# A recurrent block on 1024-column tiles: normalising ahead of the split, two-bank PSUM tiles, and pools of its own

## The chip, the cores and the metric

The kernel runs on one NeuronCore of a Trainium2 chip. Its engines are TensorE (PE; PEld is its weight load), VectorE (DVE), ScalarE (ACT) and GpSimd (POOL); SyncE (SP) issues the transfers. Time is device microseconds for one execution. Of the kernel before, three runs are known: 2192.54, 2199.36 and 2201.11 us, median 2199.36. One execution was profiled, with every instruction's start and duration.

## What is computed

Input is x, 1024 tokens of 1024 features, float32. There are two layers; each is a mixing step and an MLP, with RMSNorm ahead and a residual add behind. The change is in the first layer's mixing step, the recurrent block, and in what borders on it:

```python
def recurrent_block(x, w_in, conv_w, conv_b, w_gate, b_gate, lam, w_out):
    u = x @ w_in                                  # x already rmsnorm(x, g)
    gate, rec = u[..., :D_RNN], u[..., D_RNN:]
    rec = causal_depthwise_conv(rec, ...)         # 4 taps along the tokens
    h = rg_lru(rec, ...)
    return (jax.nn.gelu(gate) * h) @ w_out

# rg_lru, in 8 blocks of 128 features:
    r, i = sigmoid(x_block @ w_gate + b_gate), split in halves
    log_a = -8 * r * softplus(-lam);  a = exp(log_a)
    b = sqrt(-expm1(2 * log_a)) * (i * x)
    h[t] = a[t] * h[t-1] + b[t]                   # a scan along the tokens
```

The MLP is `square(relu(rmsnorm(h) @ w_up)) @ w_down`. The second layer has chunked band attention in place of the recurrent block.

## The kernel before

Features lie on the 128 partitions, tokens along the columns. A [1024 x 1024] matrix is 16 tiles of 128 x 512: k or j = 0 to 7 counts blocks of 128 features, h = 0, 1 the halves of the tokens. Every float32 product is made of three fp32r matmuls: an operand is split into a high part (ACT copies it to fp32r) and a low part (DVE or POOL subtracts), and `mm` (L321 to L323) adds high x high, high x low and low x high. A projection of one feature block is 8 k-blocks x 3 matmuls x 2 halves = 48 matmuls of 128x512. `split` (L334, L335 and, with a gain, L337, L338) splits data, `prepared` (L284, L287) the weights of the projections, `wsplit` (L732, L733) those of the MLP.

**The start** (`loads` to `first_blocks`) stands in a `manual_schedule` block: its order is written out by a small planner of the kernel (`Plan`), which starts chains of instructions as their inputs are due. x arrives as 16 tiles on SP's queue with pieces of the first two weights between them. Each tile is multiplied by the norm's gain and split as it lands (`halve`); POOL squares it. PE multiplies at once. The factor 1/rms (`R[h]`, kept negative) comes later (`rstd`) and is put on the products as they leave PSUM, so PE need not wait for it.

**The blocks.** For each n, `rec_proj` makes the recurrent half's projection, one 512-column PSUM bank per half, and a DVE instruction takes it to SBUF times -R (L556), three columns of carry ahead (L553, L555). `conv` does one tap on ACT (L572) and three on DVE (L577) per half. `gates` does the two gate products and sigmoid, tanh and exp on ACT; `lru` does the arithmetic on DVE, two products on POOL (L597, L615), a square root on ACT and the scan (L617), the second half from the first's last column. `gelu_gate` makes the other projection two blocks later, scales (L629), applies gelu, multiplies by the scan's result (L631) and splits it to `Y[n]`. `next_w` takes a prepared weight and prepares ahead. Here, and everywhere outside the `manual_schedule` blocks, the framework's planner orders each engine's instructions from the program's order, the dependences and its own cost model, and it gives each tile a buffer of its pool.

**Pools.** `gp` has 66 tiles of 128x512, `sp` 10, `wp` 16 for split weights and 8 for raw ones, `ps1` the eight PSUM banks under four tags. They are open from the first instruction to the last.

**Behind the blocks**, `Out.whole` makes the eight output blocks: a load of the residual (`first`, L674 adds it), a store of the sum to `x1d`, the square and sum for the next norm (`last`, L368 and L374), and, for each pair of blocks, `combine`, which makes the seven operand combinations `XT[0]` to `XT[6]` of the MLP. The MLP's two products are done with seven multiplications in place of eight, in 2x2 blocks. `mlp_up` asks for R first (`o.r`, whose sums on PE are L352, L353), then works through 16 steps q; `mlp_down` goes through its seven products n in the order 0, 1, 5, 4, 6, 2, 3, 16 steps q each, with operands reloaded from DRAM (`hid`), adds finished PSUM banks to x (L851), and calls `finish` on tiles that are complete. In the first layer `finish` stores x to `x2d`, squares it, adds it to the norm's sum and splits it (`done1`); in the second it only stores the output. `mlp_up`, `mlp_down` and `combine` serve both layers.

## Time and profile before

| what | value |
|---|---|
| median of three runs | 2199.36 us (2192.54 to 2201.11) |
| the profiled execution | 2197.24 us, its span 2195.5 us |
| mean granted TensorE clock | 0.983 |
| start, until the first two projections are complete | 0 to about 48 us |
| the eight blocks and the output projection | to about 347 us |
| MLP of layer 1 | to about 950 us |
| attention | about 1000 to 1500 us |
| output projection and MLP of layer 2 | to the end |

The span goes from the first to the last instruction, and some 1.7 us of the execution's time lie outside it. A stretch of the profile gives the busy time of each engine with its count of instructions; matmuls are pipelined, so their durations overlap (each is recorded with 0.39 us and more) and it is the count in a stretch that tells PE's rate. A group of instructions has the line in the kernel, the tile written, the tiles read, the shapes and the count, then busy time, mean duration in ns, and the idle time of that engine just before them with what ended it. L numbers are lines of the kernel before.

### The profile page before, as it was taken

The page shows a single profiled execution, that of the slowest core. Times are in us where ns is not written, and L with a number is a line of the kernel's source. Part 1 is how long each engine was busy: PE and PEld are TensorE (multiplying, and loading weights), DVE is VectorE, ACT ScalarE, POOL GpSimd, SP SyncE. Part 2 cuts the span into 40 slices and gives each one's busy share as a digit, 9 for nine tenths or more (in the row PEclk, how much of TensorE's full clock was granted, in tenths as well). Part 3 has the DMA queues.
Part 4 walks back from the last instruction along what each step waited for, and adds up shares of the span by engine and source line. Part 5 has one row for each costly group of instructions (what it writes and reads, how often), then busy time and mean ns, then how long its engine had stood idle before and what let it go on. Part 6 is the DMA issues. An engine that isn't in the chain of part 4 may idle for free.

```text
span 2195.5 us, 29616 instructions
## 1 busy us (share of the span) xinstructions
PE 2113.9 (96%) x9753; PEld 1741.9 (79%) x9753; DVE 1583.7 (72%) x2716; ACT 1115.1 (51%) x2030; POOL 659.8 (30%) x567
## 2 busy tenths in 40 slices
PE   7898898999999999998999999999999999999999
PEld 5676686888888888776888888878788888888887
DVE  7788867777777775554777777777677777777843
ACT  4576745443444544444666666675443443444632
POOL 5454311333320000105666656651223333000000
PEclk8999999999999999999999999999999999999999
DMA  5111144444459774343333333353354444977733
GB/s 178 37 48 37 37 141 134 163 149 149 154 196 328 241 257 134 125 144 94 90 85 87 80 80 88 92 174 111 97 184 156 152 146 153 336 262 240 255 103 99
DMA packets 176746, 319.21 MB, mean 145 GB/s; under 512 B 20816, under 2 KB 23120, under 8 KB 176592
## 3 DMA queue, kind: packets, MB, share of 16 engines
q1 hardware_dynamic: 176592, 317.33, 44.6%
q8 instruction: 76, 1.25, 0.2%
q14 instruction: 78, 0.64, 0.1%
HBM read 219.73 MB, written 78.64 MB: 136 GB/s over the span
## 4 chain that ended last, share of the span: by engine, by line
PE 77%; DVE 11%; DMA 4%; issue 3%; ACT 3%; POOL 2%; SPq 1%; DVEq 0%; POOLq 0%; ACTq 0%
PE pj L321 11%; PE pj L322 11%; PE pj L323 11%; PE tp L322 6%; PE tp L321 6%; PE tp L323 6%; PE sc L321 4%; PE sc L322 4%; PE sc L323 4%; PE tp L1172 2%; DVE c L577 2%; PE po L1200 1%; DVE l L335 1%; DMA s<-in_xT 1%; PE po L1199 1%
## 5 line engine op out<-in xcount | busy, mean ns | idle before, releaser
L321 PE MATMUL pj<-h,wh 128*128 128x512 f32 x1269 | 509.9, 402 | 8.9 <-ACT h L334 4.4
L322 PE MATMUL pj<-l,wh 128*128 128x512 f32 x1269 | 497.4, 392 | 2.9 <-DVE l L338 2.0
L323 PE MATMUL pj<-h,wl 128*128 128x512 f32 x1269 | 496.7, 392 | 0.0
L732 ACT ACTIVATE wh<-raw 128x512 fp32r<-128x512 f32 x352 | 221.6, 630 | 339.0 <-PE po L322 81.4
L733 DVE TENSOR_TENSOR wl<-raw,wh 128x512 fp32r<-128x512 f32 x352 | 277.0, 787 | 116.6 <-ACT wh L732 113.2
L321 PEld LDWEIGHTS pj<-h,wh 128*128 128x128 f32 x1269 | 239.9, 189 | 56.0 <-ACT h L334 4.9
L323 PEld LDWEIGHTS pj<-h,wl 128*128 128x128 f32 x1269 | 239.4, 189 | 51.4
L322 PEld LDWEIGHTS pj<-l,wh 128*128 128x128 f32 x1269 | 240.3, 189 | 45.8 <-DVE l L338 2.9
L321 PE MATMUL tp<-h,wh 128*128 128x512 f32 x657 | 258.4, 394 | 5.0 <-ACT h L334 4.4
L322 PE MATMUL tp<-l,wh 128*128 128x512 f32 x657 | 258.4, 393 | 2.9 <-DVE l L335 2.8
L323 PE MATMUL tp<-h,wl 128*128 128x512 f32 x657 | 257.8, 392 | 0.0
L321 PE MATMUL sc<-h,wh 128*128 128x512 f32 x569 | 224.6, 395 | 6.8 <-DVE rec L556 6.8
L322 PE MATMUL sc<-l,wh 128*128 128x512 f32 x569 | 223.9, 393 | 3.0 <-DVE l L335 3.0
L323 PE MATMUL sc<-h,wl 128*128 128x512 f32 x569 | 223.6, 393 | 0.0
L765 POOL TENSOR_TENSOR raw<-raw,raw 128x512 f32<-128x512 f32 x32 | 52.2, 1631 | 396.1 <-DVE wl L733 374.9
L335 DVE TENSOR_TENSOR l<-raw,h 128x512 fp32r<-128x512 f32 x224 | 153.2, 694 | 22.2 <-ACT h L334 20.8
L747 ACT ACTIVATE s<-s 128x512 f32<-128x512 f32 x128 | 80.3, 629 | 170.1 <-DVE s L746 170.1
L334 ACT ACTIVATE h<-raw 128x512 fp32r<-128x512 f32 x224 | 136.6, 620 | 52.9 <-DMA raw<-hid 30.9
L321 PEld LDWEIGHTS tp<-h,wh 128*128 128x128 f32 x657 | 124.7, 190 | 32.2 <-ACT h L334 5.2
L322 PEld LDWEIGHTS tp<-l,wh 128*128 128x128 f32 x657 | 124.8, 190 | 31.1 <-DVE l L335 4.8
L287 POOL TENSOR_TENSOR wl<-raw,wh 128x512 fp32r<-128x512 f32 x74 | 105.6, 1433 | 134.2 <-ACT wh L284 133.4
L323 PEld LDWEIGHTS tp<-h,wl 128*128 128x128 f32 x657 | 124.7, 190 | 26.6 <-DVE wl L733 0.6
(262 smaller groups left out, 3971.0 us busy)
## 6 DMA issues: line engine op xcount, KB each, us to landing
hid<-s SPq DMA_DIRECT2D x224, 256.0 KB, 2.0
raw<-hid SPq DMA_DIRECT2D x224, 256.0 KB, 3.7
raw<-in_w_down SPq DMA_DIRECT2D x192, 256.0 KB, 3.5
raw<-in_w_up SPq DMA_DIRECT2D x128, 256.0 KB, 2.6
s<-in_w_down SPq DMA_DIRECT2D x64, 256.0 KB, 4.4
raw<-in_w_kv SPq DMA_DIRECT2D x32, 256.0 KB, 3.5
raw<-in_w_in SPq DMA_DIRECT2D x31, 256.0 KB, 3.1
od<-ev SPq DMA_DIRECT2D x48, 128.0 KB, 2.3
```

What stands on the lines that cost most here:

```text
L287: eng.tensor_tensor(wl, raw, wh.bitcast(F32), ALU.subtract)
L321: pe.matmul(ps, lhsT=wh, rhs=xh, start=start, stop=False, skip_group_check=more)
L322: pe.matmul(ps, lhsT=wh, rhs=xl, start=False, stop=False, skip_group_check=more)
L323: pe.matmul(ps, lhsT=wl, rhs=xh, start=False, stop=stop, skip_group_check=more)
L334: act.activation(h, src, AF.Copy)
L335: dve.tensor_tensor(l, src, h.bitcast(F32), ALU.subtract)
L577: dve.scalar_tensor_tensor(ct, rec[h][:, k : k + H2], vec[:, V_CW + k, n : n + 1], ct, ALU.mult, ALU.add)
L732: act.activation(wh, raw, AF.Copy)
L733: dve.tensor_tensor(wl, raw, wh.bitcast(F32), ALU.subtract)
L747: act.activation(out, out, AF.Square)
L765: pool.tensor_tensor(raw[A11], raw[A11], raw[A21], ALU.add)
L1172: pe.transpose(pt[:, g * P : (g + 1) * P], sc[:, (kb - kb0) * P : (kb - kb0 + 1) * P], ident)
```

## The change

- The start squares the tiles on ACT, sums them on DVE as they come, and makes R of a half before that half is split. `halve` then multiplies x by R on DVE and splits the result with the gain (`gneg`, since R is negative). Three projections are made there instead of two: the recurrent blocks 0 and 1, and the gelu side of block 0. Third and further weights are loaded when the first ones are split.
- The blocks work on 1024 columns in one instruction. Their tiles come from `bp` (10 tiles of 128x1024), PSUM from `ps2` (four tiles of two banks), weights from `wpa` (10 split, 4 raw). Convolution and gelu read PSUM themselves; the scaling by R, the carries and the copies to `rec` are gone. The "+1" in `lru` goes from DVE to ACT. The scan is one instruction. The gelu side follows its block in the same step. The gelu weights' low parts are subtracted on DVE instead of POOL.
- `WideOut` is the output projection of this block on the same pools: 1024-column residual loads, squares and stores.
- These pools are closed then, and `sp`, `wp` and `ps1` are opened on the same memory, with waits tile by tile.
- `combine` splits `XT[0]` and `XT[1]` first and has one copy less. `mlp_up` asks for R after the fifth product of its first step. `mlp_down` calls `finish` for a complete product only when the operands of the first four steps of the next product stand in the program (`DEFER`).

```diff
+NB = 10
+NRAW_A = 4
+NW_A = 10
 BANKS = {"pj": 2, "tp": 3, "po": 1, "sc": 2}
-LAG = 2
-EARLY = 1
 PIN = 0
-SQA = ((6, 1), (7, 1))
 WARM = 9
-BEHIND = {(0, 0): 0, (0, 2): 1, (0, 4): 1, (1, 0): 3, (1, 4): 5}
+FIRST = 3
...
+DEFER = 3
...
-    sp = ctx.enter_context(tc.tile_pool(name="sp", bufs=NS))
-    wp = ctx.enter_context(tc.tile_pool(name="wp", bufs=NW))
     tp = ctx.enter_context(tc.tile_pool(name="tp", bufs=12))
-    ps1 = ctx.enter_context(tc.tile_pool(name="ps1", bufs=1, space=bass.MemoryType.PSUM))
     dp = ctx.enter_context(tc.tile_pool(name="dp", bufs=1, space=bass.MemoryType.DRAM))
+
+
+    first_stage = ExitStack()
+    bp = first_stage.enter_context(tc.tile_pool(name="bp", bufs=NB))
+    wp = first_stage.enter_context(tc.tile_pool(name="wpa", bufs=NW_A))
+    ps2 = first_stage.enter_context(tc.tile_pool(name="ps2", bufs=4, space=bass.MemoryType.PSUM))
+    sp = ps1 = None
+    nraw = NRAW_A
...
+    def bf(s="b", dt=F32):
+        return bp.tile([P, T], dt, tag="b", name=nm(s))
+
+    def bank2():
+        return ps2.tile([P, T], F32, tag="p", name=nm("p"))
...
-    wlist = [(w_in[NF + n], None, dve if n < 3 else pool) for n in range(max(3, 1 + EARLY))]
-    for n in range(1, NF):
-        if max(3, 1 + EARLY) <= n + EARLY < NF:
-            wlist.append((w_in[NF + n + EARLY], None, pool))
-        if n >= LAG:
-            wlist.append((w_in[n - LAG], None, pool))
-    wlist += [(w_in[n], None, pool) for n in range(NF - LAG, NF)]
+    wlist = [(w_in[NF], None, dve), (w_in[NF + 1], None, dve), (w_in[0], None, dve)]
+    for n in range(1, NF + 1):
+        if 2 <= n + 1 < NF:
+            wlist.append((w_in[NF + n + 1], None, pool))
+        if n >= 2:
+            wlist.append((w_in[n - 1], None, dve))
     wlist += [(w_out[j], None, dve) for j in range(NF)]
...
+        q = xsq[k, h] = bf("acc")[:, hs(0)]
+        act.activation(q, xin[k, h], AF.Square)
+        yield plan.use("act", c_act(H2))
+        if k:
+            yield squared[k - 1, h]
+            dve.tensor_tensor(xsq[0, h], xsq[0, h], q, ALU.add)
+            plan.use("dve", c_dve(H2))
+        squared[k, h].set(plan.t)
...
-        yield weighed[1, NF - 1]
-        yield halved[NF - 1, h]
-        a = xsq[0, h]
-        for k in range(1, NF):
-            yield squared[k, h]
-            dve.tensor_tensor(a, a, xsq[k, h], ALU.add)
-            yield plan.use("dve", c_dve(H2)) - LAT
-        yield plan.t + LAT
-        ss = bank("po")
-        pe.matmul(ss, lhsT=ones, rhs=a, start=True, stop=True)
-        yield plan.pe(4 * H2)
+        yield squared[NF - 1, h]
+        if h == 0:
+            dve.tensor_scalar(gneg, vec[:, V_AN, :], -1.0, None, ALU.mult)
+        ss = bank2()[:, hs(h)]
...
+        R[h] = r
+        normal[h].set(plan.use("dve", c_dve(H2)))
+
+    def halve(k, h):
+        yield normal[h]
+        if k:
+            yield halved[k - 1, h]
+        x = xin[k, h]
+        dve.tensor_tensor(x, x, R[h], ALU.mult)
+        yield plan.use("dve", c_dve(H2))
+        hi, lo = gr("h"), gr("l")
+        g = gneg[:, k : k + 1]
+        act.activation(hi, x, AF.Copy, scale=g)
+        X[k][h] = (hi, lo)
+        halved[k, h].set(plan.use("act", c_act(H2)))
+        yield plan.t + c_act(H2) + LAT
+        dve.scalar_tensor_tensor(lo, x, g, hi.bitcast(F32), ALU.mult, ALU.subtract)
         plan.use("dve", c_dve(H2))
-        R[h] = r
-        if h == 1:
+        if (k, h) == (NF - 1, 1):
...
+        for x in range(FIRST):
+            first_ps[x] = bank2()
         for h in range(2):
-            for x in range(2):
-                first_ps[x, h] = bank(("pj", "tp")[x])
-            if h == 0:
-                order = [(x, k) for b in range(2) for x in range(2) for k in range(4 * b, 4 * b + 4)]
-            else:
-                order = [(x, k) for k in range(NF) for x in range(2)]
-            for x, k in order:
-                yield weighed[x, k]
-                yield halved[k, h]
-                mm3(first_ps[x, h], [w[1:] for w in first_w[x]], X, h, (k,))
-                yield plan.pe(3 * H2) - LAT
+            for k in range(NF):
+                for x in range(FIRST):
+                    yield weighed[x, k // 4]
+                    yield halved[k, h]
+                    yield plan.t + c_dve(H2) + LAT
+                    mm3(first_ps[x][:, hs(h)], [w[1:] for w in first_w[x]], X, h, (k,))
+                    yield plan.pe(3 * H2) - LAT
...
+    def project(w):
+        ps = bank2()
         for h in range(2):
+            mm3(ps[:, hs(h)], w, X, h)
+        return ps
...
+    def conv(n, ps):
+        c = bf("c")
+        act.activation(
+            c, ps, AF.Identity,
+            scale=vec[:, V_CW + 3, n : n + 1], bias=vec[:, V_CB, n : n + 1],
+        )
+        for k in range(3):
+            d = 3 - k
+            dve.scalar_tensor_tensor(
+                c[:, d:], ps[:, : T - d], vec[:, V_CW + k, n : n + 1], c[:, d:], ALU.mult, ALU.add
             )
-            for k in range(1, 4):
-                dve.scalar_tensor_tensor(
-                    ct, rec[h][:, k : k + H2], vec[:, V_CW + k, n : n + 1], ct, ALU.mult, ALU.add
-                )
-            c.append(ct)
-            cs.append(split(ct))
-        return c, cs
-
-    def gates(n, gw, c, cs):
-        r, i, t = [], [], []
-        for e, dst, vb in ((0, r, V_BR), (1, i, V_BI)):
+        ch, cl = bf("ch", F32R), bf("cl", F32R)
+        act.activation(ch, c, AF.Copy)
+        dve.tensor_tensor(cl, c, ch.bitcast(F32), ALU.subtract)
+        return c, ch, cl
...
+    def gates(n, gw, c, ch, cl):
+        sig = []
+        for e, vb in ((0, V_BR), (1, V_BI)):
+            ps = bank2()
             for h in range(2):
-                ps = bank()
-                mm(ps, (gw[0][:, e, :], gw[1][:, e, :]), cs[h], True, True)
-                s = gf("sig")
-                act.activation(s, ps, AF.Sigmoid, bias=vec[:, vb, n : n + 1])
-                dst.append(s)
-        for h in range(2):
-            tt = gf("tanh")
-            act.activation(tt, r[h], AF.Tanh, scale=sp4[:, n : n + 1])
-            t.append(tt)
-            pool.tensor_tensor(i[h], i[h], c[h], ALU.mult)
-        for h in range(2):
-            act.activation(r[h], r[h], AF.Exp, scale=sp8[:, n : n + 1])
+                mm(ps[:, hs(h)], (gw[0][:, e, :], gw[1][:, e, :]), (ch[:, hs(h)], cl[:, hs(h)]), True, True)
+            s = bf("sig")
+            act.activation(s, ps, AF.Sigmoid, bias=vec[:, vb, n : n + 1])
+            sig.append(s)
+        r, i = sig
+        t = bf("tanh")
+        act.activation(t, r, AF.Tanh, scale=sp4[:, n : n + 1])
+        pool.tensor_tensor(i, i, c, ALU.mult)
+        act.activation(r, r, AF.Exp, scale=sp8[:, n : n + 1])
+        act.activation(r, r, AF.Identity, bias=ones[:, 0:1])
         return r, i, t
...
+        u = bf("q")
+        dve.scalar_tensor_tensor(u, t, 1.0, r, ALU.add, ALU.mult)
+        dve.scalar_tensor_tensor(u, u, 4.0, r, ALU.subtract, ALU.mult)
+        act.activation(t, t, AF.Sqrt, scale=0.25)
+        dve.tensor_scalar(r, u, -0.5, -1.0, ALU.mult, ALU.add)
+        dve.scalar_tensor_tensor(t, t, -1.0, u, ALU.mult, ALU.mult)
+        pool.tensor_tensor(t, t, i, ALU.mult)
+        dve.tensor_tensor_scan(u, r, t, 0.0, ALU.mult, ALU.add)
+        return u
+
+    def gelu(ps):
+        g = bf("ge")
+        act.activation(g, ps, AF.Gelu_apprx_tanh)
+        return g
+
+    def gated(n, g, hid):
+        dve.tensor_tensor(g, g, hid, ALU.mult)
+        Y[n] = [split(g[:, hs(h)]) for h in range(2)]
...
+    recs = [first_ps[0], first_ps[1]]
+    gws = {0: gate_weights(0)}
+    g0 = gelu(first_ps[2])
+    prev = (gws.pop(0), *conv(0, recs[0]))
+    for n in range(1, NF + 1):
+        if 2 <= n + 1 < NF:
+            recs.append(project(next_w()))
         if n < NF:
-            rec, gw = recs[n]
-            prev = (gw, *conv(n, rec))
-        if n > 0:
-            HS[n - 1] = lru(*rit)
-        if LAG <= n < NF:
-            gelu_gate(n - LAG)
-    for n in range(NF - LAG, NF):
-        gelu_gate(n)
+            gws[n] = gate_weights(n)
+        rit = gates(n - 1, *prev)
+        if n < NF:
+            prev = (gws.pop(n), *conv(n, recs[n]))
+        hid = lru(*rit)
+        g = g0 if n == 1 else gelu(project(next_w()))
+        gated(n - 1, g, hid)
...
-            b12, b21, b22 = sf(), sf(), sf()
+            (b12, b22), (t1, t3) = self.scratch(), self.scratch()
+            self.XT[0][i] = split(x11, ga)
+            self.XT[1][i] = split(x21, gb)
             act.activation(b12, x12, AF.Copy, scale=ga)
-            act.activation(b21, x21, AF.Copy, scale=gb)
             act.activation(b22, x22, AF.Copy, scale=gb)
-            self.XT[0][i] = split(x11, ga)
-            self.XT[1][i] = split(b21)
-            t1 = sf()
             dve.scalar_tensor_tensor(t1, x11, ga, b12, ALU.mult, ALU.subtract)
             self.XT[4][i] = split(t1)
             dve.scalar_tensor_tensor(t1, t1, -1.0, b22, ALU.mult, ALU.subtract)
             self.XT[5][i] = split(t1)
-            dve.tensor_tensor(b12, b22, b12, ALU.subtract)
-            self.XT[6][i] = split(b12)
             self.XT[2][i] = split(b22)
-            dve.scalar_tensor_tensor(t1, t1, -1.0, b21, ALU.mult, ALU.subtract)
-            self.XT[3][i] = split(t1)
+            dve.tensor_tensor(t3, b22, b12, ALU.subtract)
+            self.XT[6][i] = split(t3)
+            dve.scalar_tensor_tensor(t1, x21, gb, t1, ALU.mult, ALU.add)
+            self.XT[3][i] = split(t1, -1.0)
...
+    class WideOut(Out):
+
+
+        def scratch(self):
+            b = bf("sc")
+            return b[:, hs(0)], b[:, hs(1)]
+
+        def whole(self, Z, j0):
+            ws, pss, xs = {}, {}, {}
+            acc = bf("acc")
+            for j, h in out_order(j0):
+                if j not in ws:
+                    ws[j], pss[j] = next_w(), bank2()
+                    xs[j] = bf("xr")
+                    dma(xs[j], self.resid[j])
+                mm3(pss[j][:, hs(h)], ws[j], Z, h)
+                x = xs[j][:, hs(h)]
+                dve.tensor_tensor(x, pss[j][:, hs(h)], x, ALU.add)
+                self.XR[j][h] = x
+                if h == 0:
+                    continue
+                dma(self.keep[j], xs[j])
+                if j == 0:
+                    act.activation(acc, xs[j], AF.Square)
+                else:
+                    q = bf("sq")
+                    act.activation(q, xs[j], AF.Square)
+                    if j < NF - 1:
+                        dve.tensor_tensor(acc, acc, q, ALU.add)
+                    else:
+                        for g in range(2):
+                            self.norm.acc[g] = gf("acc")
+                            dve.tensor_tensor(self.norm.acc[g], acc[:, hs(g)], q[:, hs(g)], ALU.add)
+                if j % 2:
+                    self.combine(j // 2)
...
-        R = [o.r(0), o.r(1)]
+        R = []
...
+            if not R:
+                R.extend((o.r(0), o.r(1)))
...
+                if q == DEFER:
+                    for j0, h in left:
+                        finish(j0, h)
+                    left = []
...
-                finish(0, 0)
+                left.append((0, 0))
...
-                finish(4, 1)
+                left.append((4, 1))
             elif n == 2:
                 add(Y, 0, 1, ALU.add)
-                finish(0, 1)
+                left.append((0, 1))
...
-    o1 = Out(xT, 0, x1d)
+    o1 = WideOut(xT, 0, x1d)
     o1.whole(Y, 0)
+
+
+    first_stage.close()
+    sp = ctx.enter_context(tc.tile_pool(name="sp", bufs=NS, reuse_waits="tile"))
+    wp = ctx.enter_context(tc.tile_pool(name="wp", bufs=NW, reuse_waits="tile"))
+    ps1 = ctx.enter_context(tc.tile_pool(name="ps1", bufs=1, space=bass.MemoryType.PSUM, reuse_waits="tile"))
+    nraw = NRAW
```

148 lines of the change are left out of this document (42 added, 106 removed).

## The prediction

> **What bounds the kernel now.** I read the page first, then the busy time of each engine by stretches, then the costs of single instructions in the stretches the change touches.
>
> ```profile
> span 2195.5 us, 29616 instructions
> PE 2113.9 (96%) x9753; PEld 1741.9 (79%) x9753; DVE 1583.7 (72%) x2716; ACT 1115.1 (51%) x2030; POOL 659.8 (30%) x567
> 0.00:58.00 58.00, 45.95 (x156) 33.60 (x157) 45.72 (x63) 26.30 (x43) 32.41 (x34) 0.85 0.51 174
> 93.50:253.00 159.50, 141.49 (x587) 111.94 (x586) 138.27 (x180) 113.21 (x162) 75.04 (x46) 0.97 0.11 36
> 0.00:347.50 347.50, 309.01 (x1268) 243.67 (x1269) 278.83 (x393) 208.82 (x311) 130.10 (x95) 0.96 0.25 83
> 349.00:372.00 23.00, 16.34 (x53) 12.08 (x54) 15.99 (x23) 13.57 (x24) 5.64 (x4) 0.85 0.31 97
> 372.00:640.00 268.00, 268.00 (x1183) 221.69 (x1182) 205.14 (x275) 109.78 (x187) 91.30 (x56) 1.00 0.46 157
> 882.00:900.00 18.00, 13.33 (x46) 10.00 (x45) 17.14 (x28) 14.65 (x28) 1.50 (x2) 0.81 0.69 232
> 928.00:950.00 22.00, 16.73 (x63) 12.86 (x62) 16.18 (x26) 12.22 (x22) 0.00 (x0) 0.84 0.61 200
> 1572.00:1602.00 30.00, 23.96 (x77) 16.88 (x76) 20.71 (x32) 17.68 (x31) 6.82 (x4) 0.83 0.38 124
> ```
>
> In the window rows the columns are the stretch, its length, busy time and count of PE, PEld, DVE, ACT and POOL, the granted clock, DMA share and GB/s. PE at 96% says little, since its matmuls overlap; the counts say more. From 372 to 640 PE is never idle and does 1183 matmuls in 268 us: 0.2265 us each. That is my unit, and a stretch loses its length minus count times 0.2265. The recurrent block with its output projection is 1248 products of 128x512 (16 projections of 48, 8 gate pairs of 12, 8 output blocks of 48), 283 us of PE. With 9 idle warm-up matmuls and about 11 others these are the 1268 of the row that ends at 347.5 us, so **some 64 us are lost before 347.5**: 58 - 143 x 0.2265 = 26 us in the start, 159.5 - 587 x 0.2265 = 27 us in the 159.5 us of steady blocks, the rest around them (13 of the 156 are warm-up and norm). In the steady blocks DVE is 87% busy (138.27 of 159.5), ACT 71%, and PE waits for DVE. Four short stretches lose more: 11.0 us (349 to 372), 7.6 (882 to 900), 7.7 (928 to 950), 12.6 (1572 to 1602). Everywhere else that the change reaches PE is full, and nothing can be won.
>
> **The change, part 1: the block's instructions.** These rows price it (groups of 60 to 275 us with shapes apart, L453 from the start; the three rows with slashes give the shortest, median and longest):
>
> ```profile
> L577 DVE SCALAR_TENSOR_TENSOR c<-rec,vec,c 128x512 f32<-128x512 f32 x48 | 44.4, 926 | 1.0 <-ACT c L572 0.3
> L617 DVE TENSOR_TENSOR_SCAN q<-sig,q,tanh x8: 1267/1704/2336, 95.9 to 267.7; 128x512 f32<-128x512 f32 x8
> L615 POOL TENSOR_TENSOR tanh<-tanh,sig x16: 1257/1741/2221, 92.2 to 264.9; 128x512 f32<-128x512 f32 x16
> L556 DVE SCALAR_TENSOR_TENSOR rec<-sc,rneg x5: 659/682/691, 77.8 to 201.6; 128x512 f32<-128x512 f32 x5
> L613 DVE TENSOR_SCALAR sig<-q 128x512 f32<-128x512 f32 x16 | 6.1, 418 | 0.0
> L453 DVE TENSOR_TENSOR w<-raw,w 128x256 fp32r<-128x256 f32 x2 | 0.8, 414 | 0.0
> L335 DVE TENSOR_TENSOR l<-s,h 128x512 fp32r<-128x512 f32 x16 | 10.9, 680 | 0.0
> L562 ACT ACTIVATE gw<-graw 128x256 fp32r<-128x256 f32 x6 | 2.4, 402 | 0.0
> L334 ACT ACTIVATE h<-c 128x512 fp32r<-128x512 f32 x16 | 10.1, 631 | 41.2 <-DVE c L577 41.2
> L572 ACT ACTIVATE c<-rec,vec 128x512 f32<-128x512 f32 x15 | 12.0, 801 | 0.0
> L595 ACT ACTIVATE tanh<-sig,sp 128x512 f32<-128x512 f32 x16 | 11.0, 732 | 4.8 <-DVE q L617 2.6 <-POOL tanh L615 2.1
> L591 ACT ACT_TABLE_LOAD x8 | 10.3, 1283 | 0.1
> ```
>
> No row shows 1024 columns, so I extend the slope. DVE takes 0.414 us for 256 columns and 0.68 for 512, so 1.2 for 1024 (bounds 1.06, the slope without a fixed part, and 1.36, twice a 512). ACT: 0.402 and 0.631, so 1.09; 1.26 for the L572 kind, 1.2 for the L595 kind. The scan: 1.27 at best for 512, so 2.5.
>
> Per block DVE loses the two scalings of rec, the two of gelu, the carries, the "+1" (to ACT) and half of all fixed costs. What stays: convolution 3 x 1.2, split of c 1.2, q twice 1.2, r 0.7, tanh x q 1.2, scan 2.5, gating 1.2, two splits 1.4, its share of weight splits 1.0: **15.2 us**, where 138.27 us over 587/108 = 5.4 blocks of matmuls make 25 now. The convolution gains twice: today it reads two SBUF tensors and takes 926 ns on average, while the form that reads PSUM (L556) never leaves 659 to 691. ACT per block: 1.26 + two sigmoids 2.4 + tanh and exp 2.4 + the "+1" 1.1 + three of 1.09 + two splits 1.25 + four table loads 5.1 + weights 2.4: **19.2 us**. POOL: two 1024-wide products, 4 x 1.26 = 5.0, plus weights at the same price 2.6: 7.6 us, since seven of the thirteen remaining projections' lower parts move to DVE (in its 1.0).
>
> How much may they take? The first three projections come out of the start, so by the end of the last gate projection PE owes 1248 - 144 - 384 = 720 matmuls, 163 us, and 84 more (19 us) of the first two output blocks need no last Y. That is 182 us for eight blocks, 22.8 each. DVE (15.2) and ACT (19.2) are both below, and four two-bank tiles suffice when the convolution reads rec within a block. So PE sets the pace. Waits that remain (weights in 10 buffers rather than 16, ACT at 84%) I put at 10 us in all; bounds 3 and 34 (the last if each block took the 24.5 us of its 108 matmuls on ACT too: the last Y at 57 + 196 + 10 = 263, 24 past its cover at 57 + 182 = 239).
>
> **Part 2: the start.** Normalising first means PE gets nothing until the whole first half is summed.
>
> ```profile
> GB/s 0 0 147 270 257 295 292 249 188 169 227 314 401 402 402 415 399 388 391 388 382 388 377 375 375 382 391 377 391 388 295 148 0 0 0 0 0 0 0 0
> 48.13 0.87 PE po L493 x2
> 51.85 0.65 DVE rneg L505
> 42.94 0.43 PE tp L321
> 43.36 0.43 PE tp L322
> ```
>
> The transfers of the first 30 us, in slices of 0.75 us, bring the eight first-half tiles and the three weight pieces queued between them (11 of 256 KB, 2.9 MB) by 11.7 us. Then a square and an add (0.63 + 0.69), sum to finished norm 52.5 - 48.13 = 4.4 us, scaling and split 1.4: 18.8, and about 20 since the second half's squares (now on ACT, 0.63 each) mix in. Today PE's first product starts at 5 us. But its data trickle in; from 20 us PE has three blocks on each tile (9 matmuls, 2.0 us) against 1.4 us of DVE, with no POOL work beside it. It starts cold: after a long wait today matmuls come every 0.43 us (42.94, 43.36) for some 15 matmuls, +3 us. So 144 products end at 20 + 3 + 32.6 = 55.6, say 57 (bounds 54 and 63, the latter with all eight second-half squares ahead of the norm on ACT and the cold start doubled). Today 143 are done at 58: no gain, no loss.
>
> Stage end: 57 + 1104 x 0.2265 + 10 = **317 us against 347.5: -30** (bounds -41 and 0).
>
> **Part 3: after it.** At 1572 to 1602 the sums of squares stand ahead of the first products in PE's order (three waits there, one of the first output stage, one DMA issue):
>
> ```profile
> PE sc L352 <- ACT ah L346: 2.6, 1, 2.6
> PE po L352 <- ACT ah L346: 1.3, 1, 1.3
> PE pj L322 <- DVE l L338: 1.5, 1, 1.5
> DVE xr L674 <- DMA s<-in_xT: 15.1, 8, 2.8
> raw<-in_w_up SPq DMA_DIRECT2D x128, 256.0 KB, 2.6
> ```
>
> The change asks for R only after the fifth product and drops the copy b21. The two waits of 3.9 us go, with most of the half-speed stretch behind them; the 1.5 us wait stays. Of 12.6 us I take **-7** (bounds -2 and -10). The same loss at 349 to 372 is 11.0 us, but here new pools open on the memory of the old: the first w_up loads must wait for the tiles that lie there, and some of these live to the last combine. The residual, for which DVE waits 15.1 us today, comes in eight loads of 512 KB into ten wide tiles, early enough. I take **-4** (bounds -9 and +6; the latter if two raw tiles load only after the last combine, a 2.6 us transfer, a GpSimd add and a split later).
>
> DEFER: before the 882 us stall ACT looks like this.
>
> ```profile
> 846.37 6.11 SPq L222 DMA_DIRECT2D raw<-hid  x6
> 850.28 0.62 ACT L334 ACTIVATE h<-raw 128x512 fp32r<-128x512 f32 x1
> 881.64 0.63 ACT L368 ACTIVATE acc<-x 128x512 f32<-128x512 f32 x1 [1.36 <-DVE x L851]
> 886.33 4.25 ACT L334 ACTIVATE h<-raw 128x512 fp32r<-128x512 f32 x8
> PE tp L321 <- ACT h L334: 4.4, 1, 4.4
> ```
>
> The next product's operands are issued by 852.5, yet ACT splits none between 851 and 886: the squares and splits of finish stand first in the order, and those wait for the adds after PE's last matmul. PE then waits 4.4 us and runs half-cold. With finish behind four operands (4 x 12 matmuls, 10.9 us of PE), its eight DVE instructions (5.4 us) fit; its four x2d stores go behind these operands on SP, and nobody reads them before the attention layer. Of 7.6 + 7.7 = 15.3 us I take **-13** (bounds 0, if the order stays as it is, and -15).
>
> Sum: -30 - 7 - 4 - 13 = -54. The profiled execution took 2197.24 us (2 below the median): **2143 us**.
>
> **The rivals.**
>
> *A. Another engine sets the block's pace (0.18).* For: ACT needs 19.2 of 22.8 us, its queue is in order, and DVE and POOL stretch each other: L615 goes from 1257 to 2221 ns, L617 from 1267 to 2336. If a DVE operation with two SBUF tensors never ran beside POOL, DVE's 11 us of these and POOL's 7.6 make 18.6, still under 22.8; against: it takes further waits. At 25.5 us a block Y ends at 57 + 204 = 261, 22 past its cover at 239 instead of the 10 allowed: 2155 us. The Trainium skill (SBUF — State Buffer, section "SBUF: two separate sides") speaks for this case: the port pair that VectorE and GpSimd share is an exclusive lock held for a whole instruction, so a 1024-wide POOL product could block DVE twice as long as now. The trace agrees as far as L617's 2336 against 1267 ns shows.
>
> *B. The order edits do not do what they say (0.13).* Operands stay behind finish (0 for -13), the new pools cost 6 (for -4), R gives only -2 (for -7): +28, 2171 us. For: where instructions fall is a planner's choice; against: the 35 us in which ACT could have split and did not.
>
> *C. Slower: PE waits for a PSUM tile in every block (0.07).* Only four tiles exist; rec keeps one until all of its convolution has read it. If a projection must wait for the two sigmoids and the convolution (2.4 + 1.26 + 3.6, with hand-overs 8 us) in each of eight blocks, that is 64 us: 2143 + 64 = 2207. It turns the sign from 54/8 = 6.8 us a block. Against: rec is finished a whole projection (10.9 us) and more before its tile is asked for again.
>
> **How the numbers follow.** The forecast has 0.62. All favourable bounds together give 2197 - 75 = 2122; A and B lie at 2155 and 2171, so the range is 2118 to 2182, which leaves out C and mixtures of A with B. A measurement of this kernel tells about 0.5% from no change (2188 to 2210). Faster 0.87, within 0.06, slower 0.07.
>
> **What would show it.** Right: first product near 20 us and from then on few idle places on PE; about 1260 matmuls done by 317; DVE below 70% in the steady blocks with convolution at 1.2 us; h<-raw splits before PE ends a product of mlp_down; no 4.4 us wait at its seams. Wrong: PE waiting for conv or sigmoid in each block (C), Y later than the first two output blocks (A), w_up transfers issued only after the last combine, or a first product after 25 us.

## The result, and the profile after

The changed kernel takes 2232.07 us (median of four, 2231.35 to 2233.14), the kernel before beside it 2200.03 (four, 2192.54 to 2201.11): ratio 1.0153, 95% interval 1.013 to 1.0177. It is slower by 32 us where 54 us of gain were forecast. From here on an L number is a line of the kernel whose profile is read.

The page's first line and stretches of the changed kernel. In the cumulative rows and the two rates only PE is shown (stretch, length, PE's busy time and count, granted clock, DMA share, GB/s); the row at 93.5 has all five engines:

```profile
span 2229.6 us, 29306 instructions
0.00:58.00 58.00, 36.70 (x122) 0.79 0.40 135
93.50:253.00 159.50, 136.37 (x562) 107.62 (x561) 101.70 (x89) 109.22 (x118) 48.86 (x24) 0.95 0.12 38
0.00:260.00 260.00, 215.57 (x866) 0.92 0.19 60
0.00:350.00 350.00, 295.71 (x1198) 0.94 0.21 68
0.00:420.00 420.00, 347.85 (x1399) 0.93 0.25 83
440.00:640.00 200.00, 200.00 (x859) 1.00 0.43 147
700.00:860.00 160.00, 160.00 (x706) 1.00 0.83 275
```

The same stretches of the kernel before, where the prediction does not show them:

```profile
0.00:260.00 260.00, 225.61 (x903) 0.95 0.20 68
0.00:350.00 350.00, 309.84 (x1271) 0.96 0.25 83
0.00:420.00 420.00, 374.10 (x1534) 0.96 0.29 94
440.00:640.00 200.00, 200.00 (x884) 1.00 0.44 152
700.00:860.00 160.00, 160.00 (x707) 1.00 0.75 242
```

Two things stand in these rows.

**PE falls behind early.** Both programs issue the same kind of products, and only their count in a stretch tells progress. Against the kernel before, the changed one lacks 34 of them at 58 us, 37 at 260, 73 at 350 and 135 at 420: at 0.2266 us each it is 8, 8, 17 and 31 us behind. So the start loses 8, the blocks neither win nor lose, and the output stage with the step into the MLP loses 22. Such a count is sure to some 18 products, 4 us: the first and the fourth experiment below run the same instructions in the same order up to 420 us, and have 1390 and 1408 by then. DVE did become light: 101.70 us busy of 159.5 in the blocks, where it was 138.27. That gain reached nobody.

**PE itself is slower.** At 440 to 640 us PE is never idle in either kernel, at a granted clock of 1.00 in both, and does 859 products in place of 884: 0.2328 us each, not 0.2262. (The count of a stretch takes in the matmuls that lie across its ends; from start to start the spacing before is 0.2266 us.) At 700 to 860 both do the same. Nothing in the code of these products was changed.

What PE waited for up to 430 us, grouped by the product that stood waiting (busy time, mean ns, idle time before them and what ended it):

```profile
L332 PE MATMUL p<-h,wh 128*128 128x512 f32 x336 | 136.5, 408 | 28.5 <-ACT sig L598 14.8 <-DVE xr L735 9.2 <-ACT h L345 4.5
L332 PE MATMUL pj<-h,wh 128*128 128x512 f32 x32 | 13.6, 425 | 11.1 <-ACT wh L761 11.1
L332 PE MATMUL p<-ch,gw 128*128 128x512 f32 x32 | 13.2, 418 | 8.3 <-ACT ch L587 8.3
```

The projections wait for a sigmoid, which is not their input: they wait for its PSUM tile. The 8.3 us is a single wait, of the last block's gates for their own convolution (ch). The output blocks wait for the adds of earlier ones (xr), again for a PSUM tile; DVE's adds in turn wait 10.5 us for residuals. The first product of the MLP (pj) stands 11.1 us for its weights.

### The profile page after: what moved, and what is told of

It reads as the page before. It is cut to its first block, busy times and chain, and to the rows that moved or that the text cites. A ratio compares the mean times of both kernels' runs of the same rounds, so it can differ in the third digit from the quotient of the medians.

```text
span 2229.6 us, 29306 instructions
## 1 busy us (share of the span) xinstructions
PE 2133.3 (96%) x9753; PEld 1738.1 (78%) x9753; DVE 1533.7 (69%) x2596; ACT 1116.6 (50%) x1971; POOL 604.1 (27%) x523
## 4 chain that ended last, share of the span: by engine, by line
PE 83%; DVE 8%; ACT 4%; DMA 2%; issue 2%; POOL 1%; SPq 0%; POOLq 0%; DVEq 0%; ACTq 0%
PE pj L332 12%; PE pj L334 12%; PE pj L333 12%; PE tp L332 6%; PE tp L333 6%; PE tp L334 6%; PE sc L332 4%; PE sc L333 4%; PE sc L334 4%; PE p L332 2%; PE tp L1215 2%; PE p L333 2%; PE p L334 2%; PE po L1243 1%; PE sc L1190 1%
## 5 line engine op out<-in xcount | busy, mean ns | idle before, releaser
L332 PE MATMUL pj<-h,wh 128*128 128x512 f32 x1205 | 488.9, 406 | 11.4 <-ACT wh L761 11.1
L332 PE MATMUL tp<-h,wh 128*128 128x512 f32 x569 | 223.8, 393 | 3.0 <-ACT s L805 3.0
L333 PE MATMUL tp<-l,wh 128*128 128x512 f32 x569 | 223.6, 393 | 0.0
L334 PE MATMUL tp<-h,wl 128*128 128x512 f32 x569 | 223.6, 393 | 0.0
L332 PE MATMUL sc<-h,wh 128*128 128x512 f32 x418 | 164.4, 393 | 0.0
L333 PE MATMUL sc<-l,wh 128*128 128x512 f32 x418 | 164.4, 393 | 0.0
L334 PE MATMUL sc<-h,wl 128*128 128x512 f32 x418 | 164.3, 393 | 0.0
L345 ACT ACTIVATE h<-raw 128x512 fp32r<-128x512 f32 x224 | 137.4, 620 | 53.7 <-DMA raw<-hid 30.2
L332 PE MATMUL p<-h,wh 128*128 128x512 f32 x336 | 136.5, 408 | 28.5 <-ACT sig L598 14.8
L333 PE MATMUL p<-l,wh 128*128 128x512 f32 x336 | 135.0, 402 | 0.0
L334 PE MATMUL p<-h,wl 128*128 128x512 f32 x336 | 134.7, 401 | 0.0
```

The source lines that it names most:

```text
L332: pe.matmul(ps, lhsT=wh, rhs=xh, start=start, stop=False, skip_group_check=more)
L333: pe.matmul(ps, lhsT=wh, rhs=xl, start=False, stop=False, skip_group_check=more)
L334: pe.matmul(ps, lhsT=wl, rhs=xh, start=False, stop=stop, skip_group_check=more)
L345: act.activation(h, src, AF.Copy)
```

## The experiments

The time of each is given with its ratio to the kernel before, run on the same chip beside it. The experiments ran on four chips, so where two of them are compared across chips the ratios count as much as the times.

### Where the tiles lie

A tile lies at one byte offset in every partition, and pools follow each other in the order in which they are opened. The offsets here are worked out from the kernel's pools; the traces show no addresses. From the start of `gp` to the start of `wp` it is 66 x 2048 + 10 x 2560 = 160768 bytes in the kernel before. The change opens the tiny pool `tp` (12 tiles of 32 bytes) between the two: 161152. `gp` itself begins at byte 18784 before and, since `gneg` takes 32 bytes ahead of it, at 18816 after. The slow products are those that read the moving operand from `gp` and the weights from `wp`; at 700 to 860 both come from `wp`.

The first experiment moves one line of the changed kernel:

```diff
-    gp = ctx.enter_context(tc.tile_pool(name="gp", bufs=NG))
     tp = ctx.enter_context(tc.tile_pool(name="tp", bufs=12))
+    gp = ctx.enter_context(tc.tile_pool(name="gp", bufs=NG))
```

> The changed kernel with one line moved: the pool tp (384 bytes) is opened ahead of gp instead of behind it. The distance from gp to wp is then 160768 bytes again, as in the kernel before (161152 in the changed kernel); gp itself starts at byte 19200, where neither kernel has it. Theory 'distance': a 128x512 matmul whose moving operand lies in gp and whose weights lie in wp goes by the distance of the two. Then the spacing of those matmuls falls from 233.3 to 226.6 ns in mlp_up and the projections, and with about 6500 of them at 6.7 ns the time falls by some 43 us, to about 2189. Rival 'start of gp': it goes by where gp itself starts. Then the spacing stays at 233 ns (or takes a third value) and the time stays at about 2232. Rival 'waits': the slower spacing comes from the way the late pools wait for their tiles; then nothing changes either.

2207.51 us, ratio 1.0049 (1.0034 to 1.0064). The second leaves the order and takes the 32 bytes away:

```diff
-    gneg = cp.tile([P, NF], F32, name="gneg")
...
     e2 = cp.tile([P, NF], F32, name="e2")
+    gneg = e2
```

> The changed kernel without the 32 bytes of gneg ahead of gp (gneg shares the tile of e2, which is written later). gp starts at byte 18784 as in the kernel before; gp and wp have both moved down by 32 bytes, so their distance stays 161152. Theory 'distance': still 233.3 ns, time about 2232. Rival 'start of gp': 226.6 ns and about 2189. Rival 'waits': 233.3 ns.

2234.2 us, 1.0163 (1.0146 to 1.018). The third makes the kernel before lie as the changed one does:

```diff
     gp = ctx.enter_context(tc.tile_pool(name="gp", bufs=NG))
+    tp = ctx.enter_context(tc.tile_pool(name="tp", bufs=12))
     sp = ctx.enter_context(tc.tile_pool(name="sp", bufs=NS))
     wp = ctx.enter_context(tc.tile_pool(name="wp", bufs=NW))
-    tp = ctx.enter_context(tc.tile_pool(name="tp", bufs=12))
```

> The kernel before with one line moved: tp is opened right behind gp instead of behind wp. gp stays at 18784, sp and wp move up by 384 bytes; the distance from gp to wp becomes 161152, that of the changed kernel. Nothing else differs. Theory 'distance': mlp_up, the projections and three of the seven products of mlp_down go from 226.6 to 233.3 ns, products 0, 1, 5, 4 stay, and the time rises by some 35 to 43 us, to 2235-2243. Rival 'start of gp' and rival 'waits': 226.6 ns throughout, time 2200.

2224.17 us, 1.0122 (1.0107 to 1.0137). Stretches of the three, in this order:

```profile
0.00:420.00 420.00, 345.89 (x1390) 0.94 0.24 81
440.00:640.00 200.00, 200.00 (x884) 1.00 0.45 150
```

```profile
440.00:640.00 200.00, 200.00 (x859) 1.00 0.44 147
```

```profile
440.00:640.00 200.00, 200.00 (x862) 1.00 0.45 150
```

The count at 440 to 640 goes with the distance in all three: 884 where it is 160768, 859 and 862 where it is 161152. Where `gp` starts, and the late pools (the third kernel has none), do not matter. Nor does the place of `wp` alone: it starts at 18816 + 161152 = 179968 in the changed kernel and at 19200 + 160768 = 179968 in the first experiment, and the changed kernel's products are slow, the experiment's fast. The size was overrated: 43 us were forecast, and 25 came back by the medians (27 against the second experiment, on the same chip; 23 by the ratios); the third kernel lost 27 where 35 to 43 were forecast. The 6500 products of the expectation were too many: the changed kernel makes products of this kind almost without pause at 420 to 690, 880 to 1030, 1530 to 1910 and 2085 to 2229 us, some 4000 in all, and at 5.7 to 6.7 ns that is 23 to 27 us. Ahead of 420 nothing that can be told from scatter came back (1390 and, in the next experiment, 1408 products by then; 1399 in the changed kernel), since PE waits for others there.

### Putting off the finishes

On the kernel of the first experiment the three calls of `finish` go back to where the kernel before has them:

```diff
-                left.append((0, 0))
+                finish(0, 0)
```

and the same for (4, 1) and (0, 1).

> As the run before last but one (tiny pool first), with the three finish calls of mlp_down put back where the kernel before has them, directly behind the product, instead of three blocks later. If putting them off gained what the seams of the two profiles suggest (11 us of idle PE in the kernel before at 882-900 and 928-950, and about 4 us more behind the seams), this one is about 15 us slower than the run with tp first alone: about 2204 if that is at 2189. Rival: the seams would close anyway with the rest of the change; then no difference.

2225.55 us, 1.0137 (1.0117 to 1.0157), so the three calls are worth 18.0 us, a little over the 15 expected. Up to 420 us, and then without and with the calls put off:

```profile
0.00:420.00 420.00, 344.60 (x1408) 0.95 0.25 84
880.00:1000.00 120.00, 110.08 (x460) 0.94 0.37 119
```

```profile
880.00:1000.00 120.00, 120.00 (x531) 1.00 0.42 135
```

71 products in 120 us, 16 us, at the seams of layer 1.

### Only the edits outside the recurrent block

The kernel before, with `finish` put off in the same way, and in `mlp_up`:

```diff
-        R = [o.r(0), o.r(1)]
+        R = []
...
             product(z, 5, s2, False)
+            if not R:
+                R.extend((o.r(0), o.r(1)))
```

> The kernel before, byte for byte in its recurrent part and its pools (so its matmuls keep 226.6 ns), with only two orders of the changed kernel outside it: the three finish calls of mlp_down three blocks later, and the two norm sums behind the first block's two further products in mlp_up. Theory: these two gain by themselves what the run with tp first has gained behind 385 us: 16 to 18 us from the finishes (2225.6 against 2207.5), and 6 us plus some 3 from the norm sums in the two layers. Forecast 2197 - 18 - 8 = about 2172. Rival: the finishes only close the seams because the late pools wait tile by tile; then this gains under 10 us and stays above 2187.

2174.32 us, 0.9897 (0.9878 to 0.9917): 25 us faster than the kernel before and 58 faster than the changed one. Its counts up to 350 and 420 us, then a stretch of layer 2, here and in the kernel before:

```profile
0.00:350.00 350.00, 311.34 (x1279) 0.96 0.26 84
0.00:420.00 420.00, 375.82 (x1552) 0.96 0.29 95
1500.00:1660.00 160.00, 153.85 (x667) 0.99 0.44 147
```

```profile
1500.00:1660.00 160.00, 153.96 (x651) 0.97 0.41 140
```

At 420 us it is 18 products ahead of the kernel before, but 8 of these stood at 350, where the norm sums hardly begin, and are scatter. Product by product (the n-th matmul of one trace against the n-th of the other) the lead is 1.4 us at the end of the output stage and 4.0 at 420, 4.3 ahead of the first put-off finish and 20.9 in the attention, 21.2 ahead of layer 2's norm sums and 25.3 behind them. So the late norm sums are worth 2.5 us in layer 1 and 4.1 in layer 2, the finishes 16 to 17.

### The PSUM tiles of the blocks

How one such wait arises, in the changed kernel's timeline by engine (start, duration, instruction, idle time before it and its releaser):

```profile
118.91 2.81 DVE L616 TENSOR_TENSOR_SCAN q<-sig,tanh 128x1024 f32<-128x1024 f32 x1 [2.29 <-POOL tanh L615]
121.75 2.10 DVE L625 TENSOR_TENSOR ge<-ge,q 128x1024 f32<-128x1024 f32 x1
123.89 1.15 ACT L345 ACTIVATE h<-ge 128x512 fp32r<-128x512 f32 x2 [7.78 <-DVE ge L625]
126.87 2.12 ACT L598 ACTIVATE sig<-p,vec 128x1024 f32<-128x1024 f32 x2
128.03 0.79 PE L332 MATMUL p<-h,wh 128*128 128x512 f32 x1 [7.09 <-ACT sig L598]
```

PE has made the recurrent projection of block n+1 and both gates of n-1 by 120.9, and wants to go on with the gelu projection. All four two-bank tiles are taken: rec n (its convolution comes only behind these gates), rec n+1, r and i. The first sigmoid, which would free r, stands in ACT's queue behind a halving that waits for the scan. The Trainium skill (Perfetto Trace Analysis, section "Optimization Strategy") says that a gap that repeats on the engine that should be saturated can mean too little SBUF or PSUM for the next tile; here the five waits of 14.8 us in sum are such gaps. The experiment frees rec n earlier, on the kernel of the first experiment; tiles are named in the same order as before:

```diff
-        rit = gates(n - 1, *prev)
+        tiles = [bf(s) for s in ("sig", "sig", "tanh")]
         if n < NF:
-            prev = (gws.pop(n), *conv(n, recs[n]))
+            c0 = bf("c")
+            conv(n, recs[n], c0)
+        rit = gates(n - 1, tiles, *prev)
+        if n < NF:
+            prev = (gws.pop(n), *convsplit(c0))
```

> The run with tp first, with the convolution of block n (the ACT copy out of the PSUM tile and the three DVE steps that read it) put ahead of the gates of block n-1, so that its two-bank tile comes free earlier; the halving of c stays behind the gates. Theory 'tiles': PE waits in every block because four two-bank tiles are all held (rec n, rec n+1, r, i) when the gelu product asks for one; those waits (16 us behind sig, 7 us behind ch in the run with tp first) fall to under 10 us in sum, and the time by 8 to 15 us, to 2193-2200. Rival 'ACT and DVE chain': the tile is only the messenger, ACT and DVE come late with the chain of gates, exp and scan of the block before; then the waits move to the gates or to the last block and the time stays at 2207 or rises.

2191.66 us, 0.9964 (0.9954 to 0.9974), 16 us less (19 by the ratios).

```profile
0.00:260.00 260.00, 226.25 (x927) 0.93 0.20 64
L332 PE MATMUL p<-h,wh 128*128 128x512 f32 x336 | 135.4, 403 | 20.1 <-DVE xr L742 10.8 <-DVE c L582 4.4 <-ACT h L345 2.0
L332 PE MATMUL p<-ch,gw 128*128 128x512 f32 x32 | 12.8, 406 | 3.1 <-ACT ch L588 3.1
```

The waits for sig are nearly gone, and by 260 us PE has done 927 products, 24 more than in the kernel before in spite of the later start. The waits fell as expected, and the gain came out a little above the 8 to 15 us.

### The start

The order on ACT and PE in the changed kernel:

```profile
25.44 0.69 ACT L497 ACTIVATE rneg<-p,eps 128x512 f32<-128x512 f32 x1 [3.25 <-PE p L494]
27.36 0.70 ACT L519 ACTIVATE h<-x,gneg 128x512 fp32r<-128x512 f32 x1
28.11 0.80 PE L332 MATMUL p<-h,w 128*128 128x512 f32 x1 [2.71 <-ACT h L519]
```

The first tile of half 0 is split (h) only at 27.36, behind the norm of half 1 (rneg), which waits for a sum that PE can make when the last square of half 1 is added. On the kernel of the first experiment:

```diff
     def square(k, h):
         yield arrived[k, h]
+        if h == 1:
+            yield halved[0, 0]
...
     def rstd(h):
+        if h == 1:
+            yield halved[3, 0]
```

> The run with tp first, with the squares of half 1 held until the first tile of half 0 is normalised and the norm of half 1 until the fourth is; nothing else moves. In the profile the first normalised tile (ACT h at 26.8 us) stands in ACT's queue behind the Ln, Exp and Square of half 1, which wait for a sum that PE can only make at 22.8 us. Theory 'queue': without them the chain from the sum at 13.6 us (three ACT steps, two DVE steps, one product, one halving) ends at about 20, the first product comes 7 us earlier, and the time falls by 5 to 7 us to about 2201. Rival: the loads of half 1, the third weight block or the halving rate pace this stretch; then the first product comes earlier but the blocks start at the same time and the end stays within 2 us.

2207.43 us, 1.0039 (1.0024 to 1.0054).

```profile
19.98 0.72 ACT L523 ACTIVATE h<-x,gneg 128x512 fp32r<-128x512 f32 x1 [0.54 <-DVE x L519]
0.00:420.00 420.00, 348.56 (x1413) 0.92 0.25 84
```

The first tile is split at 19.98, the 20 us of the prediction, so the cause named is right for that instruction. PE's first product comes at 20.75, and the 144th of the start begins at 62.3 us, not at 66.1: 4 us are won there. At 420 us PE is 23 products ahead of the first experiment, but only 5 ahead of the fourth, which has the same start as the first; that is within the scatter. The expected gain of 5 to 7 us did not come (2207.51 before, the intervals of the two overlap), and the rival's "within 2 us" fits. What the start is worth at the end stays open.

### The output stage and the pools

The output stage of the kernel before, in the kernel of the first experiment; its short tiles are halves of `bp`'s:

```diff
-    o1 = WideOut(xT, 0, x1d)
+    psum_stage.close()
+    ps1 = ctx.enter_context(tc.tile_pool(name="ps1", bufs=1, space=bass.MemoryType.PSUM, reuse_waits="tile"))
+    o1 = Out(xT, 0, x1d)
```

> The run with tp first, with the output stage of the kernel before (one-bank PSUM tiles, residual and result in halves, norm sums in halves); its short-lived tiles lie in halves of the ten tiles of bp. The two-bank PSUM pool closes ahead of it, the memory of bp and wpa behind it as before. Theory: of the 39 us by which the run with tp first is late at its first w_up product (384.9 against 346.1 us), 12 come from the output stage: two-bank tiles held until the second half is added, and residual loads that wait for a bp tile. They fall away here, and the time goes to about 2196. The other 17 come from w_up loads that can't be issued until bp and wpa are free, and stay. Rival: ACT or DVE, late from the last block, pace this stage in either form; then no difference (2207).

2200.18 us, 1.0013 (1.0001 to 1.0024), 7 us less (8 by the ratios), where 12 were expected of the output stage. What PE waits for ahead of the tiles pj:

```profile
L335 PE MATMUL pj<-h,wh 128*128 128x512 f32 x68 | 27.8, 408 | 22.2 <-ACT wh L764 14.9 <-ACT h L348 7.3
```

PE's waits for xr are gone, but 14.9 us for w_up's weights and 7.3 for the last Y remain. In the changed kernel the transfers of these weights are issued only when the last output block is done:

```profile
372.57 3.69 SPq L234 DMA_DIRECT2D raw<-in_w_up  x2
382.51 0.80 PE L332 MATMUL pj<-h,wh 128*128 128x512 f32 x1 [11.07 <-ACT wh L761]
```

PE's last output product ends at 371.4 us, the first of these weights lands at 375.8, and ACT splits it only at 381.8, behind its work for the last `combine`. So some 4 of the 11 us are the late transfer itself, and the rest is the place that the late weights get in ACT's order.

The next kernel takes all these losses out together: the first experiment, the early convolution, the later squares, the old output stage, and pools in which part of the weight tiles lives from start to end while the rest takes the place of `bp` before the output stage begins:

```diff
+    wp = ctx.enter_context(tc.tile_pool(name="wp", bufs=NW_A))
     first_stage = ExitStack()
...
+    first_stage.close()
+    sp = ctx.enter_context(tc.tile_pool(name="sp", bufs=NS, reuse_waits="tile"))
+    wx = ctx.enter_context(tc.tile_pool(name="wx", bufs=NW - NW_A, reuse_waits="tile"))
     o1 = Out(xT, 0, x1d)
     o1.whole(Y, 0)
```

> The changed kernel with the four losses taken out together: tp first (distance 0 modulo 512), the convolution ahead of the gates, the squares of half 1 behind the first normalised tile, and the output stage of the kernel before with its one-bank PSUM tiles, before which bp and the two-bank pool are closed already; four raw and ten weight tiles are there from the start to the end, so w_up's first loads need not wait for the output stage. Theory (each loss has its own cause): the first w_up product, at 384.9 us with tp first alone, 368.4 with the early convolution and 346.1 in the kernel before, comes at about 335: the early convolution's 16, the start's 3 to 5, the output stage's 7 to 12, the hand-over's 15 us. From the 2192 of the early convolution that leaves about 2192 - 30 = 2160 (2152-2172). Rival: what is taken out reappears, because DVE and ACT are behind after the blocks and the output stage has to wait for the last Y and the last hidden state whatever its buffers; then no better than 2180.

2176.45 us, 0.9894 (0.9874 to 0.9914).

```profile
0.00:420.00 420.00, 377.20 (x1574) 0.94 0.30 98
L346 PE MATMUL pj<-h,wh 128*128 128x512 f32 x98 | 38.7, 395 | 12.0 <-ACT h L359 11.9
```

By 420 us it has done 175 products more than the changed kernel, 40 us, and the wait for w_up is gone. It misses the forecast of 2160 (2152 to 2172) for the reason that the rival gave, though by less than the rival's 2180: 12.0 us of waiting appear in the first output tiles, for the last Y. One more order was meant to cover these, for the first four output tiles (`head`):

```diff
+            for j, h in head:
+                pss.append(bank())
+                mm3(pss[-1], ws[j], Z, h, range(NF - 1))
+            for ps, (j, h) in zip(pss, head):
+                mm3(ps, ws[j], Z, h, (NF - 1,))
```

> The rebuilt kernel with one order changed in the first output stage: for its first four tiles PE makes the products of Y blocks 0 to 6 first (84 matmuls, 19 us) and those of block 7 behind them. In the rebuilt kernel PE stands 12.0 us at 243-255 us for the last Y. Theory: these 12 us are only the chain from the last gates to the last Y (exp, sqrt, scan, product, halving), and 19 us of other work cover it; the time falls from 2176 by 9 to 12 us, to about 2166. Rival: behind the wait stand DVE and ACT, whose work for the output tiles can't begin before Y 7 is done, so that they become the bound of the stage; then it gains under 5 us.

2181.09 us, 0.9924 (0.991 to 0.9937): no gain at all; the rival's "under 5 us" fits.

```profile
L346 PE MATMUL sc<-h,wh 128*128 128x512 f32 x64 | 26.9, 421 | 13.5 <-ACT wh L309 10.7 <-DVE xr L691 2.7
256.08 1.15 ACT L359 ACTIVATE h<-ge 128x512 fp32r<-128x512 f32 x2 [7.38 <-DVE ge L644]
258.55 3.89 ACT L309 ACTIVATE wh<-raw 128x512 fp32r<-128x512 f32 x7
```

Only 42 of the 84 products run ahead: the third output tile (sc) needs the weights of the second output block, and PE stands 10.7 us for these. ACT splits them from 258.55 on, behind the halving of the last Y at 256.08, ahead of which it sits idle for 7.38 us. So the wait for the last Y comes back by way of ACT's order. The best that was found from the changed kernel equals the small edit of the kernel before (0.9894 and 0.9897).

### Which distances are slow

The times of these two are single values; the spacing is what is read. The first gives each of 15 weight tiles 32 bytes more:

```diff
-        return wp.tile([P, H2], F32R, tag="w", name=nm(s))
+        return wp.tile([P, H2 + 8], F32R, tag="w", name=nm(s))[:, :H2]
```

> The kernel before with 15 instead of 16 weight tiles w, each followed by 32 unused bytes, so that the distance from the moving operand (gp) to the weight tile takes 15 values, 0, 32, ... 448 modulo 512 (gp's tiles and the raw tiles stay). One look at the spacing of mlp_up's matmuls by tile. Theory 'distance': the spacing is 226.6 ns for the tile at 0 and 232 to 233.5 ns for others; it shows whether every other value costs the 6.7 ns or only some. Rival: the spacing follows one or two particular values and is 226.6 ns elsewhere; 384 must be among the slow ones. The time should lie between the kernel before (2199) and the run with the tiny pool second (2224), changed a little by the missing tile.

2232.59 us.

```profile
440.00:640.00 200.00, 200.00 (x863) 1.00 0.45 150
700.00:860.00 160.00, 160.00 (x689) 1.00 0.78 246
```

Now the products at 700 to 860 are slow too, 689 for 707. By tile nothing separates: with the tiles numbered in the order in which the program asks for them (the profile names no buffers, so this is an assumption), products whose weights lie at distance 0 average 231.4 ns, the others 230.5 to 233.3. Neither theory is borne out by that. But the mean over all of them in `mlp_up`, 231.9 ns, is just the mean of the table below over these 15 distances; how it falls to single matmuls when distances are mixed stays open. The second keeps one distance through each block q of `mlp_up`:

```diff
+                woff[0] = 8 * (q if layer == 0 else NQ - 1 - q)
                 raw = [wload(w_up[layer, q, x]) for x in range(4)]
...
-        return wp.tile([P, H2], F32R, tag="w", name=nm(s))
+        return wp.tile([P, H2 + P], F32R, tag="w", name=nm(s))[:, woff[0] : woff[0] + H2]
```

> The kernel before with 12 weight tiles w of 2560 bytes instead of 16 of 2048. In mlp_up the weights of block q are put 32 q bytes into their tiles (layer 1) and 32 (15 - q) bytes (layer 2), so that within one block all weights stand at one distance from the moving operand, 0 to 480 modulo 512, and the distance changes from block to block; elsewhere they stand at 0 modulo 512 (not modulo 1024). One look at the spacing by block. Theory 'one distance for all': 226.6 ns at 0 and 233.3 ns at 384, as in the whole-kernel runs; the values between show which distances are free. Rival: in the run with 15 distances mixed even the tile at 0 had 231.4 ns, so the spacing may hang on the change of distance from one matmul to the next; then blocks with one distance are at 226.6 ns whatever it is, except that 384 contradicts it. Fewer tiles cost time elsewhere; the total is not read.

2224.54 us. First and last matmul of two stretches of layer 2 in which PE never waits, in the blocks at 256 and 32 bytes, with 53 and 52 spacings between the two:

```profile
1741.24 0.40 PE L324 MATMUL pj<-l,wh 128*128 128x512 f32 x1
1753.30 0.40 PE L323 MATMUL pj<-h,wh 128*128 128x512 f32 x1
...
1877.73 0.39 PE L324 MATMUL pj<-l,wh 128*128 128x512 f32 x1
1889.85 0.39 PE L325 MATMUL pj<-h,wl 128*128 128x512 f32 x1
```

That is 227.5 and 233.1 ns. The mean of all spacings (62 to 81) with both weights in one block:

```
distance mod 512     0     32     64     96    128    160    192    224
layer 1          228.0  233.3  233.3  234.0  232.2  233.3  228.9  233.5
layer 2          227.4  233.2  233.5  234.2  233.0  233.2  229.1  233.2
distance mod 512   256    288    320    352    384    416    448    480
layer 1          226.5  233.2  233.5  234.1  232.1  233.1  229.0  233.4
layer 2          226.7  233.2  233.5  234.1  233.0  233.2  229.2  233.2
```

The two layers went through the distances in opposite order and agree within 0.9 ns; so do the upper and the lower half of the table, within 1.5. The pattern repeats every 256 bytes: multiples of 256 are fast, 64 bytes below them nearly so, the rest cost 5 to 7 ns. The theory held at both of its values (0 and 384), and the rival falls: blocks with a single distance are slow at most distances.

## Why the prediction was wrong, point by point

Forecast 2143, measured 2232. Up to 420 us a lead of 34 us was forecast (30 from start and blocks, 4 from the step into the MLP), and the kernel is 31 behind: 65 us. Behind 420 a gain of 20 was forecast; the spans (2229.6 and 2195.5) leave a loss of 34.1 - 30.6 = 3.5: 23.5 us.

The 65 us can be read from the starts of the products in the changed kernel. The output stage ends at 371.4, not 317: 54 us. Of these the start has 9 (its 144th product begins at 66.1; 57 was the forecast). From there the 1104 products take 305 us where 1104 x 0.2265 + 10 = 260 were forecast: PE is idle for 36.7 us, not 10; 64 matmuls beside these waits come 0.32 to 0.63 us apart (0.43 for 3 to 6 us behind the longest) and cost another 12; the rest are some 6 ns apart too far, 6 us. The remaining 11 of the 65 are the step into the MLP.

- **"Everywhere else that the change reaches PE is full, and nothing can be won."** This is the step that failed behind 420 us. Nothing could be won, but something could be lost: the unit of 0.2265 us, read from the kernel before, was taken as a constant of the matmul. It hangs on where operands lie, and the pools were part of the change. The first experiment gives 23 to 27 us back, the third brings 27 into the kernel before.
- **The finishes**: the mechanism was right, the size too small: 18.0 us for a forecast of 13 (bound 15), hidden in the result by the slower rate.
- **R late**: 4.1 us at layer 2, where 7 were taken (bounds 2 and 10), measured on the kernel before; at layer 1 it is 2.5.
- **Durations of the new instructions** were right for most: the profile has 1.28 us for the convolution's steps (1.2 taken), 1.2 for its first tap on ACT, 2.3 at best for the scan (2.5). The gating product averages 2.0 where 1.2 was taken, and the 101.70 us of DVE in the row at 93.5 are about six blocks' work, some 17 us each and not 15.2. DVE's busy time fell to 64%, as "below 70%" asked, but part of that is that PE's pace fell too.
- **"Four two-bank tiles suffice when the convolution reads rec within a block", "So PE sets the pace".** This is the step that failed ahead of 420, and with it the 10 us of waits. The convolution of block n is placed behind the gates of n-1, so rec n holds its tile through them. PE waits 14.8 us in five of the blocks for a tile: rival C, given 0.07, at under a quarter of its price of 64. The same order makes the last gates wait 8.3 us for their convolution. With the convolution first the two fall to 1.2 and 3.1, with 4.4 for the convolution (c) in their place, and the blocks do win: from 58 to 260 us 807 products (927 less the 120 done by 58) against 747 in the kernel before, 14 us.
- **The start**: first product at 28.1, not 20. The rule that failed is that half 0 goes ahead when its own sum is done; ACT's queue had the norm of half 1 first. The end at 66 lies even beyond the upper bound of 63; with that order undone it is 62, so only 4 of the 9 us are explained by it.
- **"The residual ... comes ... early enough. I take -4 (bounds -9 and +6)."** Both halves failed. The output blocks wait 9.2 us for PSUM tiles and residuals; the whole output stage undone is worth 7 us. The first product of w_up waits 11.1 us: its transfers are issued at 372.57, behind the last output block, the case for which +6 was the bound.
- **Rivals A and B**: of A there is a trace, 4.5 us in which PE waits for the last Y (h L345 in the first row of PE's waits). Of B the pools came true, about 7 us for its +6; the order edits did what they say.

The rebuilt kernel recovers 40 of the 65 us; 12 more stand in its wait for the last Y. Why the other 13 are not recovered was not tested.

## What to carry to other kernels

A rate read from one profile holds for that placement of the tiles: if a change touches pools, compare the count of matmuls in a stretch where PE is full before anything else. Taking a third off the work of DVE bought nothing as long as PE waited for buffers that came free no earlier; moving the reader of a PSUM tile ahead of the next use was worth 16 us, and the whole rewriting of the blocks' instructions without that nothing between 58 and 260 us. When a big change is slow, try its small parts alone on the old kernel first: two orders outside the recurrent block were as good as the best version that was built.

## What the runs showed of the hardware

The spacing of the 128x512 fp32r matmuls of this kernel depends on the distance of their two operands in SBUF: 226.5 to 228 ns at multiples of 256 bytes, up to 234 at others. Groups at 440 to 640 us, first of the kernel before, then of the changed one:

```profile
L321 PE MATMUL pj<-h,wh 128*128 128x512 f32 x167 | 65.0, 389 | 0.0
L322 PEld LDWEIGHTS pj<-l,wh 128*128 128x128 f32 x167 | 31.3, 188 | 6.6
```

```profile
L332 PE MATMUL pj<-h,wh 128*128 128x512 f32 x163 | 64.4, 395 | 0.0
L332 PEld LDWEIGHTS pj<-h,wh 128*128 128x128 f32 x164 | 30.8, 188 | 7.5
```

The weight load keeps its 188 ns; the matmul beside it is recorded 6 ns longer (a matmul's end is modelled in the profile). That the two readings meet in the memory while the next weights are loaded is argued from this, not shown. The Trainium skill (TensorE: Matmul & The Clock Gate, section "Back-to-back issue gap") gives N / 2.4 + 2.5 ns for the isolated gap between warm matmuls, about 216 ns at 512 columns, and about 131 ns for a stream of weight loads and matmuls, both without a dependence on addresses; the traces here have 226.6 ns at best and 233 to 234 at worst, and the measurement decides.
